# A two-layer hybrid attention and MLP block on one core: w_down by seven half-size products of sums

## The chip, the core and the metric

The kernel runs on one core of a Trainium2 chip. Its engines have queues of their own: TensorE (PE in the profile, its weight loads PEld), VectorE (DVE), ScalarE (ACT), GpSimd (POOL) and SyncE (SP), which issues the transfers. The metric is the device time of one execution in microseconds (us), lower is better. Before the change it is 632.25 us, the median of 3 runs (631.75 to 632.83).

## What is computed

Two layers of a block on x with 256 rows and 1024 columns, all in float32. Each layer mixes the rows with three kinds of heads and ends with an MLP of 4096 hidden columns, squared ReLU between:

```
def hybrid_layer(x, ...):
    h = rms_norm(x, g_mix_norm)
    proj = h @ w_in
    ...                                   # mLSTM, block attention and latent attention heads -> mix
    x = x + mix @ w_out

    h2 = rms_norm(x, g_mlp_norm)
    x = x + jnp.square(jax.nn.relu(h2 @ w_up)) @ w_down
    return x
```

w_up is 1024 x 4096 and w_down 4096 x 1024. Only the product with w_down is changed.

## The kernel before

**Exact parts.** A float32 product is made of three matmuls. Each operand is held as a high part in the matmul's own format and a low part that is the rest; `mm3` (L192 to L195) multiplies high by high, low by high and high by low into the same PSUM bank. So each weight that arrives must be split: ACT copies the piece into `wh` (L182) and DVE subtracts this from the piece into `wl` (L183).

**Weight stream.** All weights come as one list of transfers of up to 1 MB (`load_plan`, L54), issued by SP into three `raw` tiles, in the order of their use. A transfer holds two pieces of 1024 columns. `stream` (L170) keeps the splits six pieces ahead of the product that asks for a piece; `wh` and `wl` have seven buffers each. A buffer is free when PE has done the last product with it, a `raw` tile when both its pieces are split.

**MLP.** The loop (L912 to L953) has 16 steps and a lag of two. Step j makes 256 hidden columns for all 256 rows: 2 blocks x 8 parts of the contraction x 3 matmuls of 256 moving columns into one bank `up` (tag `sm`, four banks). ACT takes Relu (L928) and its square, the high part `hrh` (L930); DVE makes the full square `hf` (L929) and the low part `hrl` (L931). From step 2 on the same step multiplies the hidden columns of step j - 2 with 256 rows of w_down: two blocks of 128 rows, two halves m of the rows of x, two halves n of 512 columns, 3 matmuls each, 24 matmuls of 512 columns, added up over all 16 steps in four banks `acc` (tag `big`).

**End of a layer.** With the last 256 rows of w_down the banks are finished one after the other (`last_rows`, L352): after each, DVE adds it times `r2`, the reciprocal of the mean square of a row, to its block of `xs` (L944). When three of the four blocks are done, PE transposes the first half of x for the next layer (`xtp`, L324), ACT copies the high parts `xh` (L316), DVE makes the low parts `xl` (L318), and the first products of the next layer (`latp`, L346) start while the second half is still to come. ACT also sums the squares of x there (L368). After the last layer each block goes out by a transfer.

The order of the instructions on each engine is fixed when the program is built, by a scheduler that goes by the program order and by what waits for what. At run time each engine takes its own list in that order.

Of the kernel before, what the change touches and what calls it, by code (L numbers as in the profile page):

```python
# [10 lines left out]
F32 = mybir.dt.float32  # L11
# [4 lines left out]
OP = mybir.AluOpType  # L16
# [12 lines left out]
# the stages of a layer (see "stages" in the kernel) in program order, one list for each layer  # L29
# [17 lines left out]
K_F8, K_F16, K_DIM, K_ID, K_TRI, K_NTS, K_NST, K_END = 0, 8, 24, 28, 156, 284, 412, 540  # L47

# [5 lines left out]
def load_plan(l):  # L54
    """the weights of a layer in the order of their use: one list of pieces for each transfer"""
# [14 lines left out]
    for j in range(16 + LAG):  # L70
        if j < 16:
            plan.append([("up", 2 * j), ("up", 2 * j + 1)])
        if j >= LAG:
            plan.append([("dn", 2 * (j - LAG)), ("dn", 2 * (j - LAG) + 1)])
# [13 lines left out]
def piece_cols(pc):  # L88
# [6 lines left out]
    return 1024  # L95


def pack_piece(pc, w):
# [17 lines left out]
    return w["w_down"][pc[1] * 128:(pc[1] + 1) * 128]  # L116
# [3 lines left out]
def hybrid_kernel(ctx: ExitStack, tc: tile.TileContext, x: bass.AP, xt: bass.AP, pos: bass.AP,  # L120
# [23 lines left out]
    jobs, pieces = [], []  # L144
    off = 0
    for l in range(L):
        for group in load_plan(l):
            n = sum(piece_cols(pc) for pc in group)
            c = 0
            for pc in group:  # L150
                pieces.append((l, pc, len(jobs), c, piece_cols(pc)))
                c += piece_cols(pc)
# [3 lines left out]
    raw, hl = {}, {}  # L156
    state = {"dma": 0, "split": 0}

    def load(j, cuts=1):
        """the transfer j, in as many steps as it has cuts"""  # L160
# [9 lines left out]
    def stream(i):  # L170
        while state["split"] < min(i + SPLIT_AHEAD + 1, len(pieces)):
            _, _, j, c, n = pieces[state["split"]]
# [3 lines left out]
            r = raw[j][:, c:c + n]  # L176
            if j == 0:
# [7 lines left out]
            state["split"] += 1  # L185

# [47 lines left out]
    def mask(o, j):  # L234
        """clear a bank's flags and put the additive mask mk[j] on a block of 128 columns of each head;
        what follows adds to these blocks and overwrites the rest"""
# [21 lines left out]
    def make_trig():  # L258
        """sin and cos of fl(pos * inv_freq): reduced by multiples of pi in exact steps, then a series"""
# [53 lines left out]
    def split_scaled(dh, dl, src, g):  # L313
        """parts of g * src for the blocks of one bank"""
# [13 lines left out]
    def transposer(g):  # L328
        """x transposed and times g, in two exact parts; the second half of it comes on demand"""
# [9 lines left out]
    def first_blocks(o, part, h, lo, half):  # L339
        """two blocks of a product whose input is still being made; the one start clears the bank of both;  # L340
        part(b, k): the two parts of the weights"""
# [12 lines left out]
    def last_rows(bank, update, g):  # L354
        """the last products into each bank, the update of x and the first half of its transpose"""
# [29 lines left out]
    def rotate(dst, src, tabs, half, nh, name):  # L385
        """dst, src [128, 2, nh, 2 * half]; gains are in the tables"""
# [640 lines left out]
```

## Time and profile before

| | before |
|---|---|
| median of 3 runs | 632.25 us (631.75 to 632.83) |
| span of the profiled execution, first to last instruction | 630.4 us |
| PE busy | 614.3 us, 97% |
| PEld busy | 544.8 us, 86% |
| DVE busy | 397.9 us, 63% |
| ACT busy | 334.6 us, 53% |

The span is that of one execution; the runs are timed apart from it. Busy time counts an instruction from its start to its end; matmuls overlap in the pipeline, so their starts tell the pace and their durations do not. In the order of time below, a row gives start, duration, engine, line, operation, output and inputs with shape, and how many follow each other; brackets at its end give the idle time of the engine ahead of it and what ended it.

### The profile page before, as it was taken

To read this page: it belongs to the slowest core of one execution; us is meant where nothing else is said; L and a number is where in the kernel's file an instruction comes from. 1 tells how busy PE (TensorE), PEld (TensorE's weight loads), DVE (VectorE), ACT (ScalarE), POOL (GpSimd) and SP (SyncE) were. 2 spreads that over 40 slices of the span, in tenths; PEclk is the share of its full clock that TensorE was granted. 3 is DMA by queue.
4 is the path that set the end of the run, shared out by engine and by line. 5 is a ranking of instruction groups with operands and counts; after the bars stand their busy time and mean duration, and the time that the engine had idled before them with its cause. 6 is when DMAs were issued, how large, how long until landed. Compare 5 with 4: busy or idle time off the path is not lost.

```text
span 630.4 us, 9838 instructions
## 1 busy us (share of the span) xinstructions
PE 614.3 (97%) x3850; PEld 544.8 (86%) x3850; DVE 397.9 (63%) x759; ACT 334.6 (53%) x565; POOL 40.5 (6%) x98
## 2 busy tenths in 40 slices
PE   6979999999999999999999999999999999999997
PEld 5968878889889898998889897888999898998985
DVE  4839895857555555555587997785865555555541
ACT  4864685647444444444366687554745444444430
POOL 3884000000000000000000000000000000000000
PEclk9998999999999999999999999999999999999999
DMA  8857222455546546465435623215456455464501
GB/s 274 315 189 258 77 76 92 143 191 200 176 158 205 197 163 225 148 209 192 174 108 208 237 96 129 101 67 201 153 189 213 180 198 203 142 221 172 201 2 67
DMA packets 17328, 106.39 MB, mean 169 GB/s; under 512 B 2305, under 2 KB 2817, under 8 KB 5505
## 3 DMA queue, kind: packets, MB, share of 16 engines
q1 hardware_dynamic: 17280, 105.76, 48.3%
q8 instruction: 30, 0.49, 0.3%
q14 instruction: 18, 0.14, 0.1%
HBM read 104.71 MB, written 1.05 MB: 168 GB/s over the span
## 4 chain that ended last, share of the span: by engine, by line
PE 88%; POOL 5%; DVE 3%; ACT 1%; DMA 1%; issue 1%; SPq 1%; DVEq 0%
PE acc L194 12%; PE acc L193 12%; PE acc L195 12%; PE up L193 9%; PE up L194 9%; PE up L195 9%; DVE wl L183 2%; PE vp L195 1%; PE op L193 1%; PE vp L193 1%; PE vp L194 1%; PE op L195 1%; PE op L194 1%; DMA psi<-in_pos_dram 1%; PE lsc L416 1%
## 5 line engine op out<-in xcount | busy, mean ns | idle before, releaser
L183 DVE TENSOR_TENSOR wl<-raw,wh 128x1024 fp32r<-128x1024 f32 (+2 forms) x196 | 233.4, 1207 | 142.0 <-ACT wh L182 137.7
L182 ACT ACTIVATE wh<-raw 128x1024 fp32r<-128x1024 f32 (+2 forms) x196 | 200.1, 1042 | 180.7 <-PE acc L194 93.2
L193 PE MATMUL up<-xh,wh 128*128 128x256 f32 x480 | 134.2, 280 | 0.1
L194 PE MATMUL up<-xh,wl 128*128 128x256 f32 x480 | 134.0, 279 | 0.0
L195 PE MATMUL up<-xl,wh 128*128 128x256 f32 x480 | 133.9, 279 | 0.0
L193 PE MATMUL acc<-wh,hrh 128*128 128x512 f32 x256 | 101.3, 396 | 0.0
L195 PE MATMUL acc<-wl,hrh 128*128 128x512 f32 x256 | 101.3, 396 | 0.0
L194 PE MATMUL acc<-wh,hrl 128*128 128x512 f32 x256 | 101.3, 396 | 0.0
L193 PEld LDWEIGHTS up<-xh,wh 128*128 128x128 f32 x480 | 90.2, 188 | 1.7 <-PE xtp L324 0.5
L194 PEld LDWEIGHTS up<-xh,wl 128*128 128x128 f32 x480 | 90.2, 188 | 1.2
L195 PEld LDWEIGHTS up<-xl,wh 128*128 128x128 f32 x480 | 90.2, 188 | 0.0
L195 PEld LDWEIGHTS acc<-wl,hrh 128*128 128x128 f32 x256 | 48.1, 188 | 11.5
L193 PEld LDWEIGHTS acc<-wh,hrh 128*128 128x128 f32 x256 | 48.1, 188 | 10.4
L194 PEld LDWEIGHTS acc<-wh,hrl 128*128 128x128 f32 x256 | 48.1, 188 | 10.3
L928 ACT ACTIVATE rr<-up 128x512 f32<-128x512 f32 x32 | 19.1, 596 | 52.1 <-PE up L195 52.1
L929 DVE SCALAR_TENSOR_TENSOR hf<-up,rr 128x512 f32<-128x512 f32 x32 | 22.1, 691 | 33.2 <-ACT rr L928 33.2
L193 PE MATMUL acc<-wh,mh 128*128 128x512 f32 x64 | 25.9, 404 | 0.0
L195 PE MATMUL acc<-wl,mh 128*128 128x512 f32 x64 | 25.3, 395 | 0.0
L194 PE MATMUL acc<-wh,ml 128*128 128x512 f32 x64 | 25.3, 395 | 0.0
L931 DVE TENSOR_TENSOR hrl<-hf,hrh 128x512 fp32r<-128x512 f32 x32 | 21.9, 684 | 0.1
L930 ACT ACTIVATE hrh<-rr 128x512 fp32r<-128x512 f32 x32 | 19.9, 621 | 0.0
L193 PE MATMUL qkp<-xh,wh 128*128 128x256 f32 x64 | 18.9, 295 | 0.0
(348 smaller groups left out, 961.7 us busy)
## 6 DMA issues: line engine op xcount, KB each, us to landing
raw<-in_wts_dram SPq DMA_DIRECT2D x91, 1024.0 KB, 4.8
raw<-in_wts_dram SPq DMA_DIRECT2D x2, 740.0 KB, 5.8
raw<-in_wts_dram SPq DMA_DIRECT2D x2, 576.0 KB, 5.3
xts<-in_xt_dram SPq DMA_DIRECT2D x4, 256.0 KB, 5.2
raw<-in_wts_dram SPq DMA_DIRECT2D x4, 256.0 KB, 6.1
xs<-in_x_dram SPq DMA_DIRECT2D x1, 1024.0 KB, 8.4
raw<-in_wts_dram SPq DMA_DIRECT2D x2, 512.0 KB, 3.5
raw<-in_wts_dram SPq DMA_DIRECT2D x2, 478.0 KB, 6.0
```

The source lines that it names most:

```text
L182: A.activation(h[:, :n], r, AF.Copy)
L183: V.tensor_sub(lo[:, :n], r, h[:, :n].bitcast(F32))
L193: T.matmul(o, lh, rh, start=start, stop=False)
L194: T.matmul(o, ll, rh, start=False, stop=False)
L195: T.matmul(o, lh, rl, start=False, stop=stop)
L416: T.matmul(sc[j][:, i], qT(2 * i + j, m), kT(2 * i + j, m + 1), start=False, stop=True, skip_group_check=True)
L928: A.activation(r, up, AF.Relu)
L929: V.scalar_tensor_tensor(hf, up, 0.0, r, op0=OP.max, op1=OP.mult)
L930: A.activation(hh, r, AF.Square)
L931: V.tensor_sub(hlo, hf, hh.bitcast(F32))
```

## The change

Each group of 256 rows of w_down and the hidden columns that meet it are taken as matrices of 2 x 2 blocks: the hidden ones k0m0, k0m1, k1m0, k1m1 (128 x 128 each), the weights k0n0, k0n1, k1n1, k1n0 (128 x 512 each). Instead of eight products of blocks there are seven products of sums of blocks, P1 to P7, with three matmuls each, 21 matmuls of 512 columns in place of 24. Over the 16 groups they are added up in seven PSUM banks (P1, P2 and P6 with the tag `sm`, the others `big`), so that one bank of `sm` is left to `up`. The blocks of x are put together from the banks at the end of a layer.

- A transfer for w_down is one group of 2048 columns now. Four parts of it are split: a (512 columns as they came), b (1024 as they came), c and d (1024 columns of sums each). DVE makes the sums in a tile `tsum`, in three additions of 1024, 512 and 512 columns (`dn_part`). `stream` still goes six pieces ahead, and a step has six pieces now where it had four, with the same seven buffers.
- Of the hidden columns, ACT squares all of Relu into `us`, DVE makes sums and differences in it (256, 128 and 128 columns), ACT copies the seven blocks, 896 columns, into `hrh`, and DVE subtracts into `hrl`.
- The last two groups, 14 and 15, are taken together, product by product, and DVE adds to `xs` as the banks become final: P1 and P2 into block (m 1, n 0); x1 - P6 and that + P7 as intermediate sums; these, P4, P5 and P3 into the other blocks with the sign of the formula (`nr2` is -r2).
- Transposes of the next layer's first half stand after P5 in the program.

The core of the diff (lines that only lost their comments are left out):

```diff
+DN_PARTS = {"a": 512, "b": 1024, "d": 1024, "c": 1024}
+PRODUCTS = ((1, 0, "a", 0), (2, 2, "b", 1), (6, 5, "d", 0), (7, 3, "c", 1), (4, 1, "d", 1), (5, 4, "c", 0),
+            (3, 6, "b", 0))
...
-            plan.append([("dn", 2 * (j - LAG)), ("dn", 2 * (j - LAG) + 1)])
+            plan.append([("dn", j - LAG)])
...
-    return w["w_down"][pc[1] * 128:(pc[1] + 1) * 128]
+    b = w["w_down"][pc[1] * 256:(pc[1] + 1) * 256].reshape(2, 128, 2, 512)
+    return np.concatenate([b[0, :, 0], b[0, :, 1], b[1, :, 1], b[1, :, 0]], axis=1)
...
-                pieces.append((l, pc, len(jobs), c, piece_cols(pc)))
+                if pc[0] == "dn":
+                    pieces += [(l, (*pc, part), len(jobs), 0, k) for part, k in DN_PARTS.items()]
+                else:
+                    pieces.append((l, pc, len(jobs), c, piece_cols(pc)))
...
+            if pc[0] == "dn":
+                r = dn_part(j, pc[2])
...
+    def dn_part(j, part):
+        r = raw[j]
+        if part == "a":
+            return r[:, :512]
+        if part == "b":
+            return r[:, 1024:]
+        if part == "d":
+            t = sums[j] = sb([2048], "tsum", tag="mix")
+            V.tensor_add(t[:, :1024], r[:, :1024], r[:, 512:1536])
+            V.tensor_add(t[:, 1024:1536], t[:, :512], r[:, 1024:1536])
+            V.tensor_add(t[:, 1536:], t[:, 1024:1536], r[:, 1536:])
+            return t[:, 1024:]
+        return sums.pop(j)[:, :1024]
...
-        r2 = sb([2], "r2")
-        acc = []
+        r2, nr2 = sb([2], "r2"), sb([2], "nr2")
+        prod = {}
         hs = {}
-        hrh = sb([4, 2, S], "hrh", F32R, tag="xh2")
-        hrl = sb([4, 2, S], "hrl", F32R, tag="xl2")
         rr = sb([1024], "rr", tag="dB").rearrange("p (c b t) -> p c b t", c=2, b=2)
-        hf_ = sb([2, 2, S], "hf", tag="yc")
+        us = [sb([8, 128], "us", tag=t) for t in ("yc", "qkT")]
+        hh2 = [sb([2, 7, 128], n, F32R, tag=t) for n, t in (("hrh", "xh2"), ("hrl", "xl2"))]
+        hh1 = [sb([7, 128], n, F32R, tag=t) for n, t in (("hrh", "tg"), ("hrl", "pb"))]
+        def product(p, i, first, last):
+            n, ai, part, bi = p
+            if n not in prod:
+                prod[n] = ps.tile([128, 512], F32, name=f"P{n}", tag="sm" if n in (1, 2, 6) else "big", bufs=4)
+            wh, wl = weights(l, "dn", i, part)
+            hh, hlo = hs[i]
+            c = slice(bi * 512, bi * 512 + 512)
+            mm3(prod[n], hh[:, ai], hlo[:, ai], wh[:, c], wl[:, c], first, last)
+        def into(m, n, src, sign, store=False):
+            g = (r2 if sign > 0 else nr2)[:, m:m + 1]
+            w = 256 if store and l == L - 1 and (m, n) == (1, 1) else 512
+            for c0 in range(0, 512, w):
+                c = slice(n * 512 + c0, n * 512 + c0 + w)
+                V.scalar_tensor_tensor(xs[:, m, c], src[:, c0:c0 + w], g, xs[:, m, c], op0=OP.mult, op1=OP.add)
+                if store and l == L - 1:
+                    nc.sync.dma_start(out[:, m, c], xs[:, m, c])
         for j in range(16 + LAG):
             if j < 16:
                 up = sm([2, S], "up")
                     ss2 = square_sums(xs, "ss2")
                     V.tensor_scalar(r2, ss2, 1.0 / D, EPS, op0=OP.mult, op1=OP.add)
                     V.reciprocal(r2, r2)
-                    acc = [big("acc") for _ in range(2)]
+                    V.tensor_scalar(nr2, r2, -1.0, None, op0=OP.mult)
                 else:
                     for b in range(2):
                         w = weights(l, "up", 2 * j + b)
                         for k in range(KT):
                             block(up[:, b], w, k * 128, k)
-                r, hf, hh, hlo = rr[:, j % 2], hf_[:, j % 2], hrh[:, j % 4], hrl[:, j % 4]
+                r, u = rr[:, j % 2], us[j % 2]
+                hh, hlo = [t[:, j % 3] for t in hh2] if j % 3 < 2 else hh1
                 A.activation(r, up, AF.Relu)
-                V.scalar_tensor_tensor(hf, up, 0.0, r, op0=OP.max, op1=OP.mult)
-                A.activation(hh, r, AF.Square)
-                V.tensor_sub(hlo, hf, hh.bitcast(F32))
+                A.activation(u[:, 0:4].rearrange("p (b h) t -> p b (h t)", b=2), r, AF.Square)
+                V.tensor_sub(u[:, 4:6], u[:, 1:3], u[:, 0:1].to_broadcast([128, 2, 128]))
+                V.tensor_add(u[:, 6], u[:, 4], u[:, 2])
+                V.tensor_sub(u[:, 7], u[:, 6], u[:, 3])
+                A.activation(hh, u[:, 1:], AF.Copy)
+                V.tensor_sub(hlo, u[:, 1:], hh.bitcast(F32))
                 hs[j] = (hh, hlo)
-            if j >= LAG:
-                i = j - LAG
-                ws = [weights(l, "dn", 2 * i + b) for b in range(2)]
-                def bank(n, m):
-                    down(acc[m][n], *hs[i], (0, 1), ws, m, n, i == 0, i == 15)
-                def update(n, m):
-                    w = 256 if l == L - 1 and (n, m) == NM[-1] else 512
-                    for c0 in range(0, 512, w):
-                        c = slice(n * 512 + c0, n * 512 + c0 + w)
-                        V.scalar_tensor_tensor(xs[:, m, c], acc[m][n][:, c0:c0 + w], r2[:, m:m + 1], xs[:, m, c],
-                                               op0=OP.mult, op1=OP.add)
-                        if l == L - 1:
-                            nc.sync.dma_start(out[:, m, c], xs[:, m, c])
-                if i < 15:
-                    for n, m in NM:
-                        bank(n, m)
-                else:
-                    made = last_rows(bank, update, None if l == L - 1 else pr[l + 1][:, P_MIX:P_MIX + 8])
-# ---- host side: layout only ----
+            i = j - LAG
+            if 0 <= i < 14:
+                for p in PRODUCTS:
+                    product(p, i, i == 0, False)
+        x1, u2, u3 = sb([512], "x1", tag="pa"), scratch(512), scratch(512)
+        made = None
+        for p in PRODUCTS:
+            n = p[0]
+            for i in (14, 15):
+                product(p, i, False, i == 15)
+            pn = prod[n]
+            if n == 1:
+                A.activation(x1, pn, AF.Copy)
+                into(1, 0, pn, 1)
+            elif n == 2:
+                into(1, 0, pn, 1, True)
+            elif n == 6:
+                V.tensor_sub(u2, x1, pn)
+            elif n == 7:
+                V.tensor_add(u3, u2, pn)
+                into(0, 0, u3, 1)
+            elif n == 4:
+                into(0, 0, pn, 1, True)
+                into(0, 1, u3, -1)
+                into(1, 1, u2, -1)
+            elif n == 5:
+                into(0, 1, pn, -1, True)
+                into(1, 1, pn, -1)
+                if l < L - 1:
+                    made = transposer(pr[l + 1][:, P_MIX:P_MIX + 8])
+                    made[2](0)
+            else:
+                into(1, 1, pn, -1, True)
```

Where the order of instructions moves, at three places. L183 and L202 are the same split in the two kernels, L944 and L962 the update of x, L324 and L358 the transposes.

DVE, in the even stretch of layer 0's MLP, before (two splits for `up`, two for w_down, hf and hrl):

```order
L183 TENSOR_TENSOR wl<-raw,wh 128x1024 x3
L929 SCALAR_TENSOR_TENSOR hf<-up,rr 128x512
L183 TENSOR_TENSOR wl<-raw,wh 128x1024
L931 TENSOR_TENSOR hrl<-hf,hrh 128x512
L183 TENSOR_TENSOR wl<-raw,wh 128x1024 x3
```

The same stretch after the change, one step:

```order
L215 TENSOR_TENSOR tsum<-raw 128x1024
L985 TENSOR_TENSOR us<-us 128x256
L202 TENSOR_TENSOR wl<-raw,wh 128x512
L986 TENSOR_TENSOR us<-us 128x128
L202 TENSOR_TENSOR wl<-raw,wh 128x1024
L987 TENSOR_TENSOR us<-us 128x128
L216 TENSOR_TENSOR tsum<-tsum,raw 128x512
L217 TENSOR_TENSOR tsum<-tsum,raw 128x512
L989 TENSOR_TENSOR hrl<-us,hrh 128x896
L202 TENSOR_TENSOR wl<-tsum,wh 128x1024 x2
L202 TENSOR_TENSOR wl<-raw,wh 128x1024 x2
```

A step of six operations has become one of thirteen, with the hidden sums and the sums of weights between the splits.

DVE, at the end of layer 0, before (the splits after hrl are the last of w_down and the first of the next layer):

```order
L183 TENSOR_TENSOR wl<-raw,wh 128x1024
L931 TENSOR_TENSOR hrl<-hf,hrh 128x512
L183 TENSOR_TENSOR wl<-raw,wh 128x1024 x2
L183 TENSOR_TENSOR wl<-raw,wh 128x888
L183 TENSOR_TENSOR wl<-raw,wh 128x1024
L944 SCALAR_TENSOR_TENSOR xs<-acc,r_1606,xs 128x512 x3
L318 SCALAR_TENSOR_TENSOR xl<-xtp,par_75,xh 128x256 x2
L944 SCALAR_TENSOR_TENSOR xs<-acc,r_1606,xs 128x512
```

The same place after the change, from the last two splits of w_down (from `tsum`) on; P_1859 is P6, P_1871 P7, P_1879 P4, P_1883 P5, x_3308 the copy of P1, r_1606 r2 and nr_1607 its negative:

```order
L202 TENSOR_TENSOR wl<-tsum,wh 128x1024 x2
L202 TENSOR_TENSOR wl<-raw,wh 128x1024 x3
L202 TENSOR_TENSOR wl<-raw,wh 128x888
L202 TENSOR_TENSOR wl<-raw,wh 128x1024
L1008 TENSOR_TENSOR scr<-x_3308,P_1859 128x512
L202 TENSOR_TENSOR wl<-raw,wh 128x1024
L1010 TENSOR_TENSOR scr<-scr,P_1871 128x512
L962 SCALAR_TENSOR_TENSOR xs<-scr,nr_1607,xs 128x512
L962 SCALAR_TENSOR_TENSOR xs<-scr,r_1606,xs 128x512
L962 SCALAR_TENSOR_TENSOR xs<-scr,nr_1607,xs 128x512
L962 SCALAR_TENSOR_TENSOR xs<-P_1879,r_1606,xs 128x512
L962 SCALAR_TENSOR_TENSOR xs<-P_1883,nr_1607,xs 128x512 x2
```

Six splits of the next layer's weights stand now among the operations that finish x, five of them ahead of the first.

PE, at the end of layer 0, before (`xtp`: the transposes of x, `latp`: the next layer's first product):

```order
L195 MATMUL acc<-wl,hrh 128x512
L324 MATMUL xtp<-ck,xs 128x128 x8
L193 MATMUL acc<-wh,hrh 128x512
L194 MATMUL acc<-wh,hrl 128x512
L195 MATMUL acc<-wl,hrh 128x512
L193 MATMUL acc<-wh,hrh 128x512
L194 MATMUL acc<-wh,hrl 128x512
L195 MATMUL acc<-wl,hrh 128x512
L346 MATMUL latp<-xh,wh 128x256
```

The same place after the change:

```order
L227 MATMUL P_1883<-wh,hrh 128x512
L228 MATMUL P_1883<-wh,hrl 128x512
L229 MATMUL P_1871<-wl,hrh 128x512
L229 MATMUL P_1883<-wl,hrh 128x512
L358 MATMUL xtp<-ck,xs 128x128 x8
L380 MATMUL latp<-xh,wh 128x256
L382 MATMUL latp<-xh,wl 128x256
```

Six matmuls of the last bank stood between the transposes and the next layer's product; now the last matmuls of all banks stand ahead of the transposes and none behind.

## Rows read from the trace of the kernel before

**Rows 1.** The page, part 1: busy us of each engine, share of the span, instructions
```profile
PE 614.3 (97%) x3850; PEld 544.8 (86%) x3850; DVE 397.9 (63%) x759; ACT 334.6 (53%) x565; POOL 40.5 (6%) x98
```

**Rows 2.** The page, part 4: the chain that ended last, by engine
```profile
PE 88%; POOL 5%; DVE 3%; ACT 1%; DMA 1%; issue 1%; SPq 1%; DVEq 0%
```

**Rows 3.** Waits: who for whom, us in total, times, longest
```profile
DVE wl L183 <- ACT wh L182: 137.7, 106, 3.1
```

**Rows 4.** Order of time, PE, layer 0: start us, us, engine, line, operation
```profile
159.15 0.40 PE L193 MATMUL acc<-wh,hrh 128*128 128x512 f32 x1
...
215.16 0.39 PE L193 MATMUL acc<-wh,hrh 128*128 128x512 f32 x1
...
220.76 0.28 PE L193 MATMUL up<-xh,wh 128*128 128x256 f32 x1
...
304.76 0.39 PE L193 MATMUL acc<-wh,hrh 128*128 128x512 f32 x1
```

**Rows 5.** Order of time, DVE, one step of layer 0's MLP
```profile
209.92 2.36 DVE L183 TENSOR_TENSOR wl<-raw,wh 128x1024 fp32r<-128x1024 f32 x2 [2.36 <-ACT wh L182]
...
216.93 1.23 DVE L183 TENSOR_TENSOR wl<-raw,wh 128x1024 fp32r<-128x1024 f32 x1 [0.26 <-ACT wh L182]
```

**Rows 6.** Order of time, DVE, mixers of layer 0
```profile
65.15 0.41 DVE L654 TENSOR_TENSOR lkl<-kpr,lrr_y 128x256 f32<-128x256 f32 x1
65.49 0.68 DVE L652 TENSOR_TENSOR lkl<-lkl,lks 128x512 f32<-128x512 f32 x1
66.09 0.16 DVE L308 TENSOR_TENSOR mrr_t<-mrr_y 128x16 f32<-128x16 f32 x1
66.17 1.21 DVE L183 TENSOR_TENSOR wl<-raw,wh 128x1024 fp32r<-128x1024 f32 x1
...
115.28 0.17 DVE L847 TENSOR_SCALAR ssn<-ssn 128x8 f32<-128x8 f32 x1
115.48 0.17 DVE L305 TENSOR_SCALAR nrr_i<-ssn 128x8 int32<-128x8 int32 x1
```

**Rows 7.** Order of time, ACT, one step of layer 0's MLP
```profile
215.36 0.60 ACT L928 ACTIVATE rr<-up 128x512 f32<-128x512 f32 x1 [1.74 <-PE up L195]
215.85 1.05 ACT L182 ACTIVATE wh<-raw 128x1024 fp32r<-128x1024 f32 x1
216.80 0.62 ACT L930 ACTIVATE hrh<-rr 128x512 fp32r<-128x512 f32 x1
```

**Rows 8.** Order of time, DVE, first splits after the MLP's start, both layers
```profile
148.61 1.23 DVE L183 TENSOR_TENSOR wl<-raw,wh 128x1024 fp32r<-128x1024 f32 x1 [1.75 <-ACT wh L182]
...
453.54 1.23 DVE L183 TENSOR_TENSOR wl<-raw,wh 128x1024 fp32r<-128x1024 f32 x1 [1.76 <-ACT wh L182]
```

**Rows 9.** Order of time, DVE, updates of x, end of layer 0
```profile
318.34 1.40 DVE L944 SCALAR_TENSOR_TENSOR xs<-acc,r,xs 128x512 f32<-128x512 f32 x2
320.36 0.75 DVE L944 SCALAR_TENSOR_TENSOR xs<-acc,r,xs 128x512 f32<-128x512 f32 x1 [0.62 <-PE acc L195]
```

**Rows 10.** Order of time, PE, end of layer 0
```profile
320.16 1.03 PE L324 MATMUL xtp<-ck,xs 128*128 128x128 f32 x8
...
322.43 0.28 PE L346 MATMUL latp<-xh,wh 128*128 128x256 f32 x1
```

**Rows 11.** Order of time, PE, after its longest pause
```profile
47.71 0.80 PE L195 MATMUL pp<-wl,xh 128*128 128x512 f32 x1 [4.65 <-DVE wl L183]
48.30 0.63 PE L193 MATMUL pp<-wh,xh 128*128 128x512 f32 x1
48.73 0.63 PE L194 MATMUL pp<-wh,xl 128*128 128x512 f32 x1
```

**Rows 12.** Windows: length, busy us (x) of PE PEld DVE ACT POOL, PEclk, DMA share, GB/s
```profile
47.00:50.00 3.00, 2.29 (x5) 1.83 (x6) 3.00 (x7) 0.00 (x0) 0.53 (x1) 0.50 0.10 14
50.00:53.00 3.00, 3.00 (x9) 2.32 (x8) 3.00 (x9) 0.00 (x0) 2.20 (x3) 0.50 0.99 358
```

**Rows 13.** Order of time, DVE, last update of x
```profile
626.68 0.88 DVE L944 SCALAR_TENSOR_TENSOR xs<-acc,r,xs 128x256 f32<-128x256 f32 x2 [0.65 <-PE acc L195]
```

More of the change, by code (lines that the diff above doesn't have):

```diff
@@ L94, in piece_cols @@
         return {"uq": 384, "ukv": 512}[pc[0]] * (pc[2] - pc[1])
-    return 1024
+    return 2048 if pc[0] == "dn" else 1024
 def pack_piece(pc, w):
@@ L155, in hybrid_kernel @@
     index = {(pc[0], pc[1]): i for i, pc in enumerate(pieces)}
-    raw, hl = {}, {}
+    raw, hl, sums = {}, {}, {}
     state = {"dma": 0, "split": 0}
@@ L171, in stream @@
         while state["split"] < min(i + SPLIT_AHEAD + 1, len(pieces)):
-            _, _, j, c, n = pieces[state["split"]]
+            _, pc, j, c, n = pieces[state["split"]]
             while state["dma"] < min(j + DMA_AHEAD + 1, len(jobs)):
```

## Prediction

> **What bounds the kernel now.** I read the engine shares first. TensorE (PE) is busy for 97% of the span and VectorE (DVE) for 63% [rows 1]; the chain that ended last runs over PE for 88% [rows 2]. What DVE waits for most is ScalarE's (ACT's) copy of a weight piece, 137.7 us in all [rows 3]: DVE has time to spare and stands behind ACT, and ACT behind the buffers that PE gives back. So before the change every microsecond of MLP matmul is a microsecond of the kernel. The second view is PE's order of time in the MLP. The first product group with w_down starts at 159.15 and the fourteenth at 304.76, so a step takes 145.61 / 13 = 11.20 us, without a hole; its 24 down matmuls take 5.60 us (215.16 to 220.76), 0.233 each, and the 48 up matmuls the other 5.60 [rows 4]. The third is DVE's order of time: in such a step it runs six operations, four splits (wl), hf and hrl, and idles 2.36 us ahead of the first pair alone [rows 5].
>
> **What is removed.** Seven products of three matmuls instead of eight: 3 x 0.233 = 0.70 us a step, a PE step of 10.50, and over 32 steps 22.4 us. That is all the change can bring, and only where PE is what ends last.
>
> **What is added, engine by engine.** A DVE operation costs the next one its start-to-start time, which is shorter than its duration: 1024 columns start 1.14 apart (the pair of 2.36 us less one duration of 1.23 or a little under) [rows 5], 512 columns 0.60, 256 columns 0.34, 16 columns 0.08 [rows 6]; between these I take 0.20 for 128 and 1.00 for 896. An operation that needs the result of the one just ahead of it starts 0.20 after it where 0.08 would do, so it adds 0.12 [rows 6]. DVE's step after the change holds the two up splits, the splits of the parts b, d and c and the first sum of weights (six of 1024: 6.84), the split of a and two more sums (three of 512: 1.81), the hidden sums (0.34 + 0.20 + 0.20) and hrl over 896 columns (1.01): 10.4 us, 10.41 in the sums below. Before it was 4 x 1.14 + 2 x 0.60 = 5.8. No row shows these sums of weights, but they have the shape and types of rows that stand there. ACT's operations start 0.49 (512) and 0.95 (1024) apart [rows 7], so 0.84 for 896: five copies of 1024, the part a, Relu, Square and the copy of 896 make 5 x 0.95 + 3 x 0.49 + 0.84 = 7.1 us, not a bound. The transfers keep their bytes, their number and their queue.
>
> So DVE, 10.41, and PE, 10.50, are level, and what decides is the waits inside DVE's order. From the order of the changed kernel: after the last hidden sum (call its start 0) ACT copies hrh from 0.32 and cannot begin the d copy before the third sum of weights is written, 1.60; that copy ends at 2.68, DVE's split of d starts at 2.72, while its own queue was free at 2.53. That is 0.19, and 0.12 for the third sum behind the second: a DVE step of 10.71. Two early steps stand in another order and wait 0.49 for hrh. DVE then loses about 0.2 us a step against PE. Seven weight buffers, which were almost two steps of pieces and are now just over one (six pieces a step instead of four), leave PE some 4 us of slack, so PE still goes at 10.50 through the fourteenth group, which I put at 159.15 + 13 x 10.50 = 295.65, 9.1 us early.
>
> **The end of a layer is where it is paid.** Groups 14 and 15 are pulled together, eight pieces for seven buffers, and DVE must first finish all that it is behind with. I count DVE as one chain. It starts the stream at about 148.6, where a split stands now on the same freed buffer [rows 8]. Ahead of it: sixteen steps of 10.41 less 9.8 already done (six up splits, part a, the first sums) plus two updates of x at 0.65 (two in 1.40 us, one of 0.75 [rows 9]): 158.1 us. The waits by hand through the order: 2.6 in the first steps (Square, the c copy, hrh, the buffer that the first P3 frees), 4.0 in the even stretch (two of 0.49, ten of 0.30), 2.4 at the end (d of 14, then the three sums of 15 behind the updates, the d copy). The last split of w_down is done at 148.6 + 158.1 + 9.0 = 315.7, and PE's last products with it near 316. PE alone would be there at 310.5.
>
> In layer 0 DVE's order then puts five pieces of the next layer (4 x 1.14 + 1.00) ahead of the first difference x1 - P6 (0.60), another piece (1.14), then P7's sum (0.60), three updates from SBUF (1.80) and the update with P4 (0.75): 10.4 us, until 326.1. Only then is the (0, 0) block of x whole, and PE's queue has the transposes of x next: it stands for some 10 us. ACT's sum of squares, now ahead of the copies of xh, waits for the (0, 1) block as well (0.7), takes 1.05, the first xh 0.48: the first product of layer 1 starts at 328.3. Before, the transposes at 320.16 lay between products and this product started at 322.43 [rows 10]. Layer 0 ends 5.9 us **late**. [...]
>
> In layer 1 the stream starts 304.93 later [rows 8], so the last split is done at 620.6. No next layer stands in between: ten operations follow, 0.60 + 0.72 + 3 x 0.60 + 3 x 0.65 + 0.52 + 0.48 = 6.1, and the last half of x is written at 626.7; before it was 626.68 + 0.88 = 627.56 [rows 13]. So 0.9 early. The one bank left to `up` (P1, P2 and P6 keep three of four) I cost at nothing: Relu empties it in 0.6 us beside 4.9 us of products; if ACT comes over 4.3 us late, that cover is gone.
>
> **Sum.** +5.9 + 2.0 - 0.9 = +7.0 us on the profiled span of 630.4: 637.4. The median of the runs, 632.25, is 1.85 above that span; I carry this over: **639.2 us**.
>
> **Rivals.**
> 1. *The matmuls alone count.* If DVE kept its cover to the end: 632.25 - 22.4 = 609.9. For it: PE 97%, DVE 63%. Against it: 10.41 against 10.50 in a step, and operations of DVE that stand between the last product and the transposes. [...] Chance 0.03.
> 2. *Faster, since DVE waits less.* One place: the hand-overs between DVE and ACT. Nine us of waits a layer are my own count; each us less moves both layers, and the clock's 2.0 stays. At 3.5 us less a layer the change is even, at 6 less it is 639.2 - 12 = 627.2. For it: half of the nine are waits of 0.1 to 0.5 us by hand, and a split that is late leaves ACT time to run ahead. Against: the pieces of layer 1 ahead of the update, with no wait at all in them, are 10.4 us. Chance of faster here 0.06, of within the bound 0.09.
> 3. *DVE's operations do not overlap.* Then each of the 13 costs its duration, 0.08 more, about 1.05 a step: DVE at 11.8 is slower than the old step, PE waits in every step, 2 x 15 x 1.05 = 31 more: 670. The pair of 2.36 speaks against it [rows 5]. [...] Chance 0.03.
> 4. *The step stalls earlier.* If DVE's waits grow by 0.3 a step, the slack is used up and both ends move by 3.5 to 4: 646. It is the upper end of my forecast and in its chance.
>
> **How the numbers follow.** My case, with its spread of waits, 0.79; rival 2 0.15; rivals 1 and 3 0.03 each. Range: from waits 3.5 us a layer smaller, 632.2, rounded to 632, to 646, rival 4; this leaves out about 0.2. A measurement here can tell about 0.2%, 1.3 us, from no change. Faster: 0.03 + 0.06 = 0.09. Within: 0.09. Slower: 0.79 + 0.03 = 0.82.
>
> **What the profile would show.** Right: 672 product matmuls instead of 768 at the same 0.233 apart; a step of 10.5 in PE's order of time and DVE busy without holes over 0.5 us; PE idle for 8 to 11 us ahead of the transposes at the end of layer 0, released by DVE, with the granted clock at 0.5 after it; DVE the last engine for about 6 us at the end. Wrong: DVE idle in the even stretch waiting for PE's `up` (then it has room and the end is cheap); a step over 10.8 (then PE waits within the steps); no pause ahead of the transposes, which would take the largest term away.

## The result and the profile after

The changed kernel takes **639.52 us** (median of 4 runs, 637.70 to 640.25) beside 632.18 us before (now 4 runs; the first 3 gave 632.25): a ratio of 1.0109, 95% interval 1.0094 to 1.0125, 7.3 us slower. It was forecast at 639.2. The profiled execution is the fastest of the four: its span is 635.8 us, 5.4 more than before, while the spans of the other three are 637.4 to 638.2.

The page of the kernel after, busy time of each engine, answers to [rows 1]:

```profile
PE 600.2 (94%) x3754; PEld 535.0 (84%) x3754; DVE 549.0 (86%) x999; ACT 408.6 (64%) x663; POOL 40.8 (6%) x98
```

PE has 96 matmuls and 14.1 us less, DVE 151 us more: from 63% of the span to 86%. The chain that ended last, by engine, answers to [rows 2]:

```profile
PE 79%; DVE 9%; POOL 5%; ACT 2%; issue 2%; DMA 1%; SPq 1%; DVEq 0%; ACTq 0%
```

DVE's share went from 3% to 9%, and PE's from 88% to 79%: at the end of both layers (from about 293 to 326 us, and from 604 us on) the chain now runs over DVE and ACT. The waits after (who for whom, us in all, times, longest) answer to [rows 3]:

```profile
ACT hrh L988 <- DVE us L987: 62.8, 24, 3.1
DVE wl L202 <- ACT wh L201: 34.6, 48, 2.8
ACT wh L201 <- DVE tsum L217: 20.9, 22, 3.6
```

Before, DVE stood behind ACT for 137.7 us. Now ACT stands behind DVE: for the hidden sums (L987) and for the third sum of weights (L217). PE's order of time in layer 0, answering to [rows 4]: the first and the fourteenth product group, and between them the `up` matmuls of one step and the group behind them:

```profile
158.42 0.40 PE L227 MATMUL P<-wh,hrh 128*128 128x512 f32 x1
...
205.44 0.28 PE L227 MATMUL up<-xh,wh 128*128 128x256 f32 x1
...
211.19 0.40 PE L227 MATMUL P<-wh,hrh 128*128 128x512 f32 x1
...
295.73 0.40 PE L227 MATMUL P<-wh,hrh 128*128 128x512 f32 x1
```

A PE step is (295.73 - 158.42) / 13 = 10.56 us, and PE waits nowhere in this stretch. The 48 `up` matmuls take 5.75 us (205.44 to 211.19) where they took 5.60 before. DVE's first split of the stream, answering to [rows 8], and its order of time in the even stretch of layer 0, one step from split to split, answering to [rows 5]:

```profile
148.13 1.23 DVE L202 TENSOR_TENSOR wl<-raw,wh 128x1024 fp32r<-128x1024 f32 x1 [1.59 <-ACT wh L201]
...
197.32 2.36 DVE L202 TENSOR_TENSOR wl<-tsum,wh 128x1024 fp32r<-128x1024 f32 x2 [0.18 <-ACT wh L201]
...
205.48 0.68 DVE L216 TENSOR_TENSOR tsum<-tsum,raw 128x512 f32<-128x512 f32 x1
206.20 0.69 DVE L217 TENSOR_TENSOR tsum<-tsum,raw 128x512 f32<-128x512 f32 x1
...
208.08 2.36 DVE L202 TENSOR_TENSOR wl<-tsum,wh 128x1024 fp32r<-128x1024 f32 x2 [0.18 <-ACT wh L201]
```

A DVE step is 208.08 - 197.32 = 10.76 us. The two small losses that were priced stand in it: 0.18 in brackets ahead of the split of d, and the third sum starting 0.72 after the second, on which it depends, instead of 0.60. The end of layer 0 on DVE, answering to [rows 9]:

```profile
312.12 2.36 DVE L202 TENSOR_TENSOR wl<-tsum,wh 128x1024 fp32r<-128x1024 f32 x2 [1.12 <-ACT wh L201]
314.40 5.62 DVE L202 TENSOR_TENSOR wl<-raw,wh 128x1024 fp32r<-128x1024 f32 x5
319.93 0.68 DVE L1008 TENSOR_TENSOR scr<-x,P 128x512 f32<-128x512 f32 x1
...
324.25 0.74 DVE L962 SCALAR_TENSOR_TENSOR xs<-P,r,xs 128x512 f32<-128x512 f32 x1
```

And the same place on PE, answering to [rows 10]:

```profile
312.14 0.79 PE L227 MATMUL P<-wh,hrh 128*128 128x512 f32 x1 [2.85 <-ACT wh L201]
...
316.13 0.62 PE L229 MATMUL P<-wl,hrh 128*128 128x512 f32 x2
325.14 1.94 PE L358 MATMUL xtp<-ck,xs 128*128 128x128 f32 x8 [8.39 <-DVE xs L962]
327.25 0.58 PE L380 MATMUL latp<-xh,wh 128*128 128x256 f32 x1 [0.17 <-ACT xh L350]
...
330.14 1.03 PE L358 MATMUL xtp<-ck,xs 128*128 128x128 f32 x8
```

The last splits of w_down come 1.12 late behind ACT's copies of the same sums, for which PE has stood 2.85 us. Then DVE does five splits of the next layer (5.62) before it touches x1 - P6, and PE stands 8.39 us. Two windows behind that, in the form of [rows 12]:

```profile
320.00:325.00 5.00, 0.00 (x0) 0.00 (x0) 5.00 (x9) 0.94 (x1) 0.00 (x0) 0.50 0.80 275
325.00:330.00 5.00, 4.69 (x23) 4.33 (x24) 4.93 (x11) 3.64 (x8) 0.00 (x0) 0.58 0.18 70
```

The granted clock (third number from the end) is 0.50 in this part of the pause and up to 329 us, 0.88 from there to 330 and 1.00 from 330 to 335; between 150 and 300 us it is 1.00. The end of layer 1 on DVE, answering to [rows 13]:

```profile
623.25 2.36 DVE L202 TENSOR_TENSOR wl<-tsum,wh 128x1024 fp32r<-128x1024 f32 x2 [1.12 <-ACT wh L201]
626.53 0.69 DVE L1008 TENSOR_TENSOR scr<-x,P 128x512 f32<-128x512 f32 x1 [0.92 <-PE P L229]
...
630.70 2.31 DVE L962 SCALAR_TENSOR_TENSOR xs<-P,nr,xs 128x512 f32<-128x512 f32 x4
```

### The profile page after: what moved, and what is told of

It reads as the page before. It is cut to its first block, busy times and chain, and to the rows that moved or that the text cites. A ratio compares the mean times of both kernels' runs of the same rounds, so it can differ in the third digit from the quotient of the medians.

```text
span 635.8 us, 9983 instructions
## 1 busy us (share of the span) xinstructions
PE 600.2 (94%) x3754; PEld 535.0 (84%) x3754; DVE 549.0 (86%) x999; ACT 408.6 (64%) x663; POOL 40.8 (6%) x98
## 4 chain that ended last, share of the span: by engine, by line
PE 79%; DVE 9%; POOL 5%; ACT 2%; issue 2%; DMA 1%; SPq 1%; DVEq 0%; ACTq 0%
PE up L227 9%; PE up L229 9%; PE up L228 9%; PE P L227 7%; PE P L228 7%; PE P L229 7%; DVE wl L202 4%; PE acc L229 2%; PE acc L227 2%; PE acc L228 2%; ACT wh L201 2%; DVE xs L962 2%; PE vp L229 1%; PE op L227 1%; PE vp L227 1%
## 5 line engine op out<-in xcount | busy, mean ns | idle before, releaser
L202 DVE TENSOR_TENSOR wl<-raw,wh 128x1024 fp32r<-128x1024 f32 (+3 forms) x196 | 215.2, 1117 | 30.6 <-ACT wh L201 26.4
L201 ACT ACTIVATE wh<-raw 128x1024 fp32r<-128x1024 f32 (+3 forms) x196 | 185.3, 969 | 64.1 <-PE acc L228 18.7
L227 PE MATMUL P<-wh,hrh 128*128 128x512 f32 x224 | 90.2, 403 | 6.1 <-ACT wh L201 6.0
L228 PE MATMUL P<-wh,hrl 128*128 128x512 f32 x224 | 89.2, 398 | 0.0
L229 PE MATMUL P<-wl,hrh 128*128 128x512 f32 x224 | 86.7, 394 | 1.0 <-DVE wl L202 1.0
L202 DVE TENSOR_TENSOR wl<-tsum,wh 128x1024 fp32r<-128x1024 f32 x64 | 75.8, 1221 | 8.2 <-ACT wh L201 8.2
L201 ACT ACTIVATE wh<-tsum 128x1024 fp32r<-128x1024 f32 x64 | 64.5, 1050 | 21.7 <-DVE tsum L217 20.9
L227 PEld LDWEIGHTS P<-wh,hrh 128*128 128x128 f32 x224 | 43.1, 192 | 17.2 <-ACT wh L201 9.2
L229 PEld LDWEIGHTS P<-wl,hrh 128*128 128x128 f32 x224 | 42.5, 190 | 11.8 <-DVE wl L202 2.3
L228 PEld LDWEIGHTS P<-wh,hrl 128*128 128x128 f32 x224 | 43.0, 192 | 7.8
```

The costliest lines, as they stand in the source:

```text
L201: A.activation(h[:, :n], r, AF.Copy)
L202: V.tensor_sub(lo[:, :n], r, h[:, :n].bitcast(F32))
L227: T.matmul(o, lh, rh, start=start, stop=False)
L228: T.matmul(o, ll, rh, start=False, stop=False)
L229: T.matmul(o, lh, rl, start=False, stop=stop)
```

## The experiments

The theory is that the matmuls saved are worth their 22.4 us, and that DVE, made as busy as PE, gives them back: by its waits in the steps, and by its queue at the end of a layer. The rivals are that the matmuls or the added DVE work cost something else than priced, that buffers, the one bank for `up` or the two groups taken together stall the end, and that the clock is the price.

**1. The matmuls alone.** The kernel before, with one of eight products left out:

```diff
...
-                    down(acc[m][n], *hs[i], (0, 1), ws, m, n, i == 0, i == 15)
+                    down(acc[m][n], *hs[i], (0, 1), ws, m, n, i == 0, i == 15,
+                         (0, 1) if (n, m) != (1, 0) else (0,) if i == 0 else (1,))
```

> The kernel before, with one of the eight block products of every group of w_down left out (3 of 24 matmuls; that part of the result is missing) and nothing added on DVE. Theory: PE bounds the kernel before and 0.233 us go with each matmul, 32 x 0.70 = 22.4: 609.8 us (608 to 612), a step of 10.50, the ends of the layers as before. Rival (the matmuls are not worth their time, so the seven products could never have paid): 625 or more.

Measured: **610.22 us** beside 632.5, ratio 0.9645 (0.9631 to 0.966), 22.3 us. The term of the matmuls is right to 0.1 us, and it is all there when DVE has room and the rest of the kernel stays as it was.

**2. The DVE work alone.** The kernel before, eight products, with four operations added behind hrl (256, 128, 128 and 384 columns) and four in each group (1024, 512, 512, 1024):

```diff
+                V.tensor_sub(du[:, 0:256], hf[:, 0], hf[:, 1])
...
+                if i < 15:
+                    V.tensor_add(dt[:, :1024], xs[:, 0], xs[:, 1])
...
```

> The kernel before with all eight products and 4.7 us of additions on DVE added to each of its steps (of the shapes of the sums of weights, of hidden columns and of the longer hrl; nobody reads them), none with the last group of a layer. Theory: DVE's step of about 10.5 lies under PE's 11.2, so it costs little: 632 to 634. Rival (the added DVE work costs by itself, through hand-overs to ACT or slower operations, whatever PE does): 0.2 us a step and more, 638 or later.

Measured: **632.3 us** beside 632.5, ratio 0.9996 (0.9986 to 1.0005). DVE is 84% busy instead of 63%, and it costs nothing, since a DVE step of 10.5 lies under a PE step of 11.2. Nothing waits for these additions, so this tests DVE's time and not the hand-overs. Neither half of the change loses anything by itself; what loses is that a DVE step of 10.76, its waits included, meets a PE step of 10.56.

**3. Without the sums of weights.** The changed kernel, with d and c split from raw columns:

```diff
-            t = sums[j] = sb([2048], "tsum", tag="mix")
-            V.tensor_add(t[:, :1024], r[:, :1024], r[:, 512:1536])
...
-            return t[:, 1024:]
-        return sums.pop(j)[:, :1024]
+            return r[:, 512:1536]
+        return r[:, :1024]
```

> The changed kernel without the three sums of weights: the parts d and c are split from the raw columns, so the result is another. DVE's step falls by 2.3 us to 8.1. Theory (DVE level with PE is the cause): DVE keeps ahead, PE goes at 10.5 to the end of each layer, the pause ahead of the transposes shrinks from 8.4 us to 1 to 3, and most of the 22.4 us appears: 614 us (611 to 618). Rivals (one bank for up, seven buffers for eight pieces, the two last groups together): these all stay, so it would be above 630.

Measured: **623.95 us**, ratio 0.986 (0.9846 to 0.9875): 15.6 us less than the changed kernel. The bank, the buffers and the pairing all stay, so they are not the cause of these 15.6 us. But it is 10 us more than I expected, and the pause hardly shrank. DVE and PE at the end of layer 0 of this kernel, in order of time:

```profile
309.27 3.35 DVE L202 TENSOR_TENSOR wl<-raw,wh 128x1024 fp32r<-128x1024 f32 x3
...
314.92 1.22 DVE L202 TENSOR_TENSOR wl<-raw,wh 128x1024 fp32r<-128x1024 f32 x1
316.06 0.68 DVE L1006 TENSOR_TENSOR scr<-scr,P 128x512 f32<-128x512 f32 x1
```

```profile
311.44 0.39 PE L225 MATMUL P<-wl,hrh 128*128 128x512 f32 x1
319.54 1.94 PE L354 MATMUL xtp<-ck,xs 128*128 128x128 f32 x8 [7.71 <-DVE xs L958]
```

PE is through with the products at 311.5, about where PE alone was put (310.5). Still it stands for 7.71 us (8.39 in the changed kernel): DVE's order has the next layer's splits ahead of x1 - P6 and of P7's sum here too, and with DVE in time they simply start earlier. So the order at the end of the layer looks like a second cause, apart from the backlog; experiments 4 and 10 test it.

**4. The order at the end alone.** The changed kernel; DVE's halves of the next layer's splits are kept in a list and written behind the updates:

```diff
...
-                V.tensor_sub(lo[:, :n], r, h[:, :n].bitcast(F32))
+                held.append((lo[:, :n], r, h[:, :n].bitcast(F32)))
+                if not state["hold"] or pieces[state["split"]][1][0] in ("up", "dn"):
+                    flush()
...
                 into(0, 0, pn, 1, True)
+                flush(2)
                 into(0, 1, u3, -1)
...
```

> The changed kernel with DVE's splits of the next layer held back at the end of layer 0 until the blocks of x that the first transposes need are written; ACT's copies stay where they are. Theory (five splits, 5.6 us, ahead of x1 - P6 delay the transposes): transposes at about 320 instead of 325.1; some of the splits held back are then waited for, so 3 to 5 us of the 7.3 come back: 635.5 us (634 to 637). Rival (the lateness is set before, in the steps, and the splits are only moved): 639, the first product of layer 1 at 327 as now.

Measured: **633.96 us**, ratio to before 1.0025 (1.0015 to 1.0036): 5.6 us less than the changed kernel, a little more than the 3 to 5 expected. PE at the end of layer 0:

```profile
321.21 1.67 PE L366 MATMUL xtp<-ck,xs 128*128 128x128 f32 x8 [3.59 <-DVE xs L970]
```

The pause is 3.59 us instead of 8.39; the stream of this execution had started 1.1 us later (149.23 instead of 148.13).

**5. The sums of weights on GpSimd**, `V.tensor_add` to `G.tensor_add` in the three lines of `dn_part`.

> The changed kernel with the three sums of weights made by GpSimd (POOL), which idles in the MLP, instead of DVE; nothing is left out. Theory (DVE level with PE is the cause): DVE's step falls to 8.1 us, and the time is that of the kernel without the sums, 624 us (621 to 628), if POOL makes the three in less than a step. POOL's longest tensor operations in the trace of before, of 48 to 96 columns, take 0.35 to 0.5 us, so 2048 columns are not known from it: I put them at 3 to 8 us. Rival (POOL is too slow or slows DVE's operations): POOL over 10.5 us a step or splits well over 1.22 us, and the time at 640 or later.

**6. The same with the order of experiment 4.**

> The sums of weights on POOL and the next layer's DVE splits held back at the end of layer 0, together; nothing is left out. Theory: the two causes are separate, and without the sums PE was done with the products at 311.5 and then stood for 7.7 us behind seven splits; with these behind x, the pause falls to 1 to 2 us: 618 us (615 to 621), if POOL keeps up. Rival (both repair the same loss): no better than the better one of the two, 624 or later.

Measured: **702.32 us** (ratio 1.1104, 1.1087 to 1.112) and **695.77 us** (1.1, 1.0981 to 1.1018). The rival holds in both. POOL and DVE of the first one in order of time:

```profile
197.80 3.27 POOL L215 TENSOR_TENSOR tsum<-raw 128x1024 f32<-128x1024 f32 x1 [5.51 <-DVE wl L202]
201.14 2.16 POOL L216 TENSOR_TENSOR tsum<-tsum,raw 128x512 f32<-128x512 f32 x1
203.38 1.63 POOL L217 TENSOR_TENSOR tsum<-tsum,raw 128x512 f32<-128x512 f32 x1
210.52 3.26 POOL L215 TENSOR_TENSOR tsum<-raw 128x1024 f32<-128x1024 f32 x1 [5.52 <-DVE wl L202]
```

```profile
197.58 6.27 DVE L202 TENSOR_TENSOR wl<-raw,wh 128x1024 fp32r<-128x1024 f32 x3
203.77 1.51 DVE L985 TENSOR_TENSOR us<-us 128x256 f32<-128x256 f32 x1
...
208.03 2.35 DVE L202 TENSOR_TENSOR wl<-tsum,wh 128x1024 fp32r<-128x1024 f32 x2
```

POOL needs 7.2 us for the three (197.80 to 205.01), which would fit. (Single POOL operations on 48 and 96 columns had taken up to 1.3 us in the trace before, more than the expectation says.) But while it works, three splits of DVE take 6.27 us where three take 3.5 (a pair of 2.36 and 1.14 more), and the operation on 256 columns 1.51 where it takes 0.42 in the changed kernel; when POOL is done, two splits take 2.35 again. A step is 210.52 - 197.80 = 12.72. The order of experiment 4 is worth 6.6 us here as well.

**7. PE kept busy in the pause**, with 34 matmuls that nobody reads:

```diff
...
-                    made[2](0)
+                    dm = sm([4, 128], "dm")
+                    with tc.issue_after(lastp[0].ins):
+                        for _ in range(NDUMMY):
+                            d = T.matmul(dm, identb, mk[:, 0:1].to_broadcast([128, 4, 128]), start=True,
+                                         stop=True, skip_group_check=True)
+                    with tc.issue_after(d.ins):
+                        made[2](0)
```

> The changed kernel with 34 matmuls of 512 columns that nobody reads put on PE between the last product of layer 0 and the transposes, some 7.5 us, so that PE does not stand still; DVE's order is the same up to the transposes. ACT's first sum of squares also falls behind the first xh, which alone takes 1.2 us from the path. Theory (the pause lowers the clock, which costs 1 to 2 us): granted clock 1.0 after the transposes, first products 0.12 apart and not 0.21, and with ACT's 1.2 together 2 to 3 us back: 637 us (636 to 638). Rival (the clock costs nothing of itself, the products then wait for DVE's xl anyway): 638.3 or later with the clock at 1.0.

Measured: **636.31 us** (ratio 1.0062, 1.0047 to 1.0077), 3.2 less than the changed kernel. The window 325 to 330 and the first products:

```profile
325.00:330.00 5.00, 4.19 (x33) 3.96 (x34) 5.00 (x9) 2.60 (x6) 0.00 (x0) 1.00 0.31 131
```

```profile
325.68 1.09 PE L359 MATMUL xtp<-ck,xs 128*128 128x128 f32 x8 [2.42 <-DVE xs L963]
326.90 0.38 PE L381 MATMUL latp<-xh,wh 128*128 128x256 f32 x1
...
328.92 0.27 PE L359 MATMUL xtp<-ck,xs 128*128 128x128 f32 x1
```

With the clock at 1.00 the sixteen first products take 2.02 us (326.90 to 328.92); in the changed kernel they took 2.89 (327.25 to 330.14). So the clock costs 0.9 us behind the pause. Another 0.9 lies between the transposes and the first product (2.11 there, 1.22 here): xh no longer stands behind ACT's square (1.06 there), and the eight transposes run faster too (1.09 instead of 1.94), which this run does not separate. Where the rest of the 3.2 came from, the two traces do not settle.

**8. Groups 14 and 15 one after the other.**

```diff
-            if 0 <= i < 14:
+            if 0 <= i < 15:
...
-            for i in (14, 15):
+            for i in (15,):
```

> The changed kernel with the last two groups one after the other instead of product by product; DVE's order is the same. Theory (DVE's backlog sets the end, not the eight pieces for seven buffers): same within 1 us, 639 (638 to 641). Rival (pulling the groups together costs the stall of 2.85 us ahead of the last products in each layer): 634 to 636.

Measured: **640.24 us**, ratio 1.012 (1.0105 to 1.0135): no change. PE's stand ahead of its last products stays too (3.04 us), so the pairing and its eight pieces for seven buffers cost nothing that can be seen.

**9. The sums of weights earlier.** The three additions are written with the part a instead of with the part d:

```diff
         if part == "a":
+            t = sums[j] = sb([2048], "tsum", tag="mix")
+            V.tensor_add(t[:, :1024], r[:, :1024], r[:, 512:1536])
+            V.tensor_add(t[:, 1024:1536], t[:, :512], r[:, 1024:1536])
+            V.tensor_add(t[:, 1536:], t[:, 1024:1536], r[:, 1536:])
             return r[:, :512]
...
-            t = sums[j] = sb([2048], "tsum", tag="mix")
...
-            return t[:, 1024:]
+            return sums[j][:, 1024:]
```

> The changed kernel with the three sums of weights asked for with the part a instead of with the part d, so that ACT can copy d and c without waiting for the third sum; the same operations, nothing left out. Theory (the waits of 0.18 and 0.12 us a step ahead of the d split, 2.4 at the end of a layer, are what puts DVE behind PE): 3 to 4 us less in each layer, 632.5 us (631 to 635), no idle time of DVE ahead of the d split. Rival (DVE's operations alone fill the step, the waits are replaced by others): 638 to 640.

Measured: **628.06 us**, ratio 0.9928 (0.9911 to 0.9945): 11.5 us less than the changed kernel and faster than the kernel before, by the same operations in another order. That is 4.4 us better than expected, and below the stated range. DVE at its first split, in one step and at the end of each layer, and PE's pause:

```profile
149.47 1.23 DVE L202 TENSOR_TENSOR wl<-raw,wh 128x1024 fp32r<-128x1024 f32 x1 [1.71 <-ACT wh L201]
...
180.83 1.22 DVE L211 TENSOR_TENSOR tsum<-raw 128x1024 f32<-128x1024 f32 x1
...
191.31 1.22 DVE L211 TENSOR_TENSOR tsum<-raw 128x1024 f32<-128x1024 f32 x1
...
310.61 5.62 DVE L202 TENSOR_TENSOR wl<-raw,wh 128x1024 fp32r<-128x1024 f32 x5
...
616.86 0.68 DVE L1008 TENSOR_TENSOR scr<-x,P 128x512 f32<-128x512 f32 x1
```

```profile
321.35 1.94 PE L358 MATMUL xtp<-ck,xs 128*128 128x128 f32 x8 [9.52 <-DVE xs L962]
```

The step is 10.48 us instead of 10.76, without a bracket: just under PE's 10.56 where it was just over it. What went is the wait for ACT's copy; a sum still starts 0.11 late behind the one it needs. The five splits of the next layer start at 310.61 instead of 314.40, but this execution's stream had also started 1.3 us later: counted from their first splits, layer 0 takes 161.1 us (149.47 to 310.61) instead of 166.3 (148.13 to 314.40), 5.1 less, and layer 1's stretch shrinks by the same. At the end of layer 1 x1 - P6 follows the last split at once, where DVE waited 0.92 us for PE in the changed kernel, because PE no longer stands for the last splits. In layer 0 PE's pause is even longer, 9.52 us: with DVE in time PE is done earlier, and the next layer's splits still stand ahead of x.

**10. Both, and the held splits pinned behind the update with P4**, so that none stands between x1 - P6 and that update.

> Early sums, and the next layer's DVE splits held back at the end of layer 0, here pinned behind the update with P4 (before, two of them had come ahead of P7's sum and of the updates); nothing left out. Theory (both losses are separate): from 633.96 with the order alone, 6 to 8 us less by the waits and 2 by the pinned splits: 625 us (622 to 629), faster than the kernel before. Rival (the waits and the order repair the same loss): 632 or later.

Measured: **621.29 us**, ratio 0.9824 (0.981 to 0.9839): 11.1 us faster than the kernel before and 18.2 faster than the changed kernel, a little below the range expected. DVE and PE at the end of layer 0:

```profile
307.73 2.35 DVE L211 TENSOR_TENSOR wl<-tsum,wh 128x1024 fp32r<-128x1024 f32 x2
309.99 0.68 DVE L1018 TENSOR_TENSOR scr<-x,P 128x512 f32<-128x512 f32 x1
...
313.40 0.75 DVE L970 SCALAR_TENSOR_TENSOR xs<-P,r,xs 128x512 f32<-128x512 f32 x1
```

```profile
314.29 1.93 PE L366 MATMUL xtp<-ck,xs 128*128 128x128 f32 x8 [3.06 <-DVE xs L970]
```

The two repairs add up: 11.5 and 5.6 are 17.0 of the 18.2 us, so they are two causes. The other 1.2 came with the pinned splits, which no run has alone.

**11. PE kept busy in the short pause** of experiment 10, with 10 such matmuls; the orders of DVE and ACT are the same.

> The kernel with early sums and the held splits (621.29 us), with 10 matmuls of 512 columns that nobody reads (2.2 us) put on PE into its pause of 3.06 us ahead of the transposes at the end of layer 0; DVE's and ACT's orders are the same. Theory A (the lower clock after a pause has a price of its own): granted clock 1.0 instead of 0.73 from 315 to 320, the first products 0.12 apart, 1 to 1.5 us less: 620.0 (619.6 to 620.4). Theory B (DVE's chain to the second half of x sets the end there, its last update ended at 319.95 and PE's second transposes waited for it): the clock is 1.0 and the time within 0.5 us of 621.3.

**12. The same with 6, and the first block of x finished earlier**, by two updates moved behind the one with P4.

> As the run before this one with 6 such matmuls, and two updates of the other blocks of x (0.66 us each) moved behind the update with P4, so that the first transposes come 1.3 us earlier; nothing left out. Theory A: 1 to 1.3 us less than that run: 619 (618.5 to 619.5). Theory B (the second half of x comes no earlier): within 0.5 us of it.

Measured: **621.59 us** (ratio 0.9833, 0.9817 to 0.9849) and **622.24 us** (0.9842, 0.9826 to 0.9859). The first is theory B. The second is 0.65 above the first, just past the 0.5 of theory B and on the far side from theory A: nothing was gained. The window of experiment 11 and PE's second transposes:

```profile
315.00:320.00 5.00, 4.43 (x30) 3.63 (x30) 5.00 (x9) 2.72 (x6) 0.00 (x0) 1.00 0.30 83
```

```profile
321.02 0.87 PE L367 MATMUL xtp<-ck,xs 128*128 128x128 f32 x6 [0.21 <-DVE xs L971]
```

The clock is at 1.00 (0.73 in the same window of experiment 10), and the time is the same, 621.59 beside 621.29 us: PE reaches the second half of x and waits 0.21 us for DVE's last update, as it did in experiment 10. Here the lower clock cost nothing, since DVE came later anyway.

## Why the prediction was right, point by point

- **PE's step, 10.50.** The first product group stands at 158.42 and the fourteenth at 295.73 (forecast 295.65): 10.56 a step. That the fourteenth is where I put it is luck: the first was 0.7 earlier, and thirteen steps were 0.06 longer each. The 22.4 us were there to be had in experiment 1, where the step is 10.50. In experiments 3, 9 and 10 it is 10.56 as well, so neither the sums of weights nor DVE's waits make the difference; it lies in the `up` matmuls (5.75 for 5.60, while the products took 4.8 for 4.9), and its cause is open. The one bank left to `up`, which I cost at nothing, was not tested alone.
- **DVE's step, 10.71.** Measured 10.76, with the 0.18 and the 0.12 at their places. These waits, small as they are, were the right thing to price: with the sums asked for earlier (experiment 9), which takes out the wait for the copy in the steps and that at the end of a layer, the kernel is 11.5 us faster.
- **The last split of w_down, 315.7; PE's last products, 316; PE alone, 310.5.** Measured 314.4, 316.1 and, in experiment 3, 311.5. The stream started at 148.13 instead of 148.6, and from there the work and the waits took 166.3 instead of the 167.1 counted.
- **Ten us of DVE ahead of the transposes.** From the last split to the transposes 10.7 us (314.40 to 325.14; 10.4 forecast), from there to the first product 2.1 (2.2). Layer 0 ends 4.8 us late (327.25 against 322.43), not 5.9: the last split was 1.3 earlier, the operations behind it 0.3 longer.
- **The clock, 2.0.** No run shows this term. In its place the runs showed about half: the second transposes are 5.84 late (330.14 against 324.30 before), so 1.0 was added between the first product and them, and experiment 7 measures 0.9. The matmuls that pay have 256 columns: from 327.62 to 329.12 they start 0.21 apart, in experiment 7 0.12.
- **Layer 1, -0.9.** The end is 5.45 late on the spans' scale (633.01 against 627.56), so layer 1 gave 0.4 back. The term that was missing is PE at the end of layer 1: after its 2.83 us of standing its matmuls started 0.43 apart (granted clock 0.50 from 623 to 626), and DVE waited 0.92 and 0.23 us for its last products, which I had put earlier. Part of this was made up by the splits, which took 0.8 less than counted, as in layer 0.
- **The sum, +7.0.** On the profiled execution it is +5.4, on the medians +7.3. The agreement of 639.2 with 639.5 is thus better than its terms, and in part luck: in the profiled execution two were too large by 1.1 and 1.0, one too small by 0.5. This execution is 1.8 us under the median; experiment 8, with the same order on DVE and a span of 638.5, starts the stream at 149.06 and reaches the transposes at 326.39 and the first product at 328.50, where the forecast had 326.1 and 328.3. Why the stream starts anywhere from 148.1 to 149.5 in the executions shown here is open.

**The rivals.** The first (609.9) is what experiment 1 gives, and not what a kernel gives that needs the sums. The second, fewer waits, had the right place: it was the sensitive term, each us of waits counting in both layers, but the kernel as it stood did have the waits; my 627.2 for it is near the 628.06 of experiment 9. The third falls with the starts 1.14 apart inside the pair of 2.36. Of the fourth, a stall of the steps, nothing is seen: PE does not wait between 150 and 300 us. The signs came out as well: a pause of 8.39 us released by DVE, the clock at 0.50 for 3.9 us after it (325.14 to 329), DVE last for 5.4 us at the end.

**Where the gain went, in one sum.** From the changed kernel's 639.5 to the 610.2 of the matmuls alone are 29.3 us. The sums of weights asked for late are 11.5 of them, the next layer's splits ahead of x 5.6, and 1.2 came with the pinned splits. What is left, 621.3 against 610.2, is 10.3 us in the spans of the traces of experiments 10 and 1. Of these 4.0 lie between the fourteenth group of layer 0 and the first product of layer 1 (19.6 us instead of 15.6), with the pause of 3.06 us in them, 4.3 between the fourteenth group of layer 1 and the end of the last update (20.1 instead of 15.8), where ten operations of DVE follow the last split, and 1.6 in the steps of 10.56 instead of 10.50; the rest is elsewhere.

## What to carry to other kernels

When work moves from the bounding engine to another, put the two steps side by side, with the waits between the engines in them: here, with two steps within 3% of each other, a hand-over of 0.2 us a step became the bound. Then look at the ends, where the engine that has become late meets the next stage: work for the next stage that is queued ahead of the result that this stage needs is paid for there. Both were cured here by order alone (ask for an operand earlier, hold back what nobody needs yet), and this is worth trying before arithmetic is taken back.

## What the runs showed of the hardware

- VectorE was slower while GpSimd added: beside POOL's additions the splits of 1024 columns started 2.1 us apart instead of 1.14, and 1.14 apart again when POOL was done (experiment 5). From 197.58 to 205.32 are 7.74 us, of which DVE's three splits and the 256 columns would take 3.8 alone (3 x 1.14 + 0.34, an estimate from their starts without POOL); what POOL's sums take alone, and what makes DVE slower beside them, no run here shows.
- Two pauses of PE of one length were not followed by the same clock. In the changed kernel PE stood for 2.85 us between 308.9 and 312.1, and the matmuls behind this started 0.43 apart; in experiment 7 it stood for 2.83 us at the same place, and they started 0.23 apart. The windows from 310 to 315 of the two (granted clock third from the end: 0.72, which is 1.00 up to 312, 0.59 from there to 313 and 0.50 from 313 on, and 1.00):

```profile
310.00:315.00 5.00, 2.86 (x7) 2.29 (x8) 3.88 (x5) 3.97 (x5) 0.00 (x0) 0.72 0.59 198
```

```profile
310.00:315.00 5.00, 2.23 (x10) 1.72 (x10) 3.88 (x5) 3.34 (x4) 0.00 (x0) 1.00 0.44 147
```
